# A two-layer decoder trunk: gate projection joined to the value projection, filler rewoven, low halves of weight splits put later

## The chip, the cores and the metric

The kernel runs on one core of one Trainium2 chip. The metric is the device time of one launch in microseconds; several runs of the same kernel are summed up by their median. The profile is one further execution, recorded by the hardware profiler, and its times count from the first instruction of the span. PE is the matrix engine, PEld its weight loads, DVE the vector engine, ACT the scalar engine, POOL the general engine, and SP the engine from whose queue most DMAs are issued.

## The reference, cut to what matters

The trunk has two layers over 512 tokens of width 1024, all in 32-bit floats. Each layer is a mixer, a residual with layer norm, an expert-retrieval feed-forward (PEER, dense over 16384 experts in this kernel), and a second residual with layer norm.

```python
# layer 1, mixer A
proj = x @ w_in                                        # 1024 x (384 q, 384 k, 768 v, 768 r, 16 glr, 256 qm)
log_g = log_sigmoid(glr @ w_gate2 + b_gate) / 16       # low-rank forget gate, rank 16
o = gla_chunked(q / 8, k, v, log_g)                    # 6 heads, chunks of 64 tokens
o = o * rsqrt(mean(o**2) + eps) * head_g * silu(r)
m = softmax(qm @ km.T / 8) @ vm                        # 4 heads over 256 memory tokens; km, vm from mem @ w_mem_kv
mix = concat(o, m) @ w_out
# layer 2, mixer B
q, qm = split(x @ w_in)                                # 12 query heads of 64, 4 memory heads
k, v = split(h @ sb_w_kv)
o = stick_breaking(q, k, v)                            # strictly causal, blocks of 128
mix = concat(o, memory_attention(qm)) @ w_out
```

## The kernel before, in words

**Splits.** A projection in 32-bit floats is made of three matrix products. `split` (line 85) takes a 128 x 1024 weight tile `raw`; ACT copies it, rounded, to `hi`, and DVE subtracts to get `lo`. The tokens x are held in the same way, transposed, as `xhi` and `xlo`: 128 x 8 chunks of the width x 512 tokens. Each block of a product is then hi by hi, hi by lo and lo by hi, accumulated in one PSUM bank. `split` takes an optional list `later`, into which the DVE subtraction is put as a function instead of being issued.

**Two kinds of projection.** `stat_mm` (line 108) holds 128 output columns of the weight and streams tokens: 8 chunks x 3 = 24 matmuls of 512 tokens, the output transposed. `nat_units` (line 154) holds 128 tokens and streams weight columns, with four accumulators for the four token tiles; one `yield` is one unit, that is one 128 x 1024 weight tile. For 512 columns a unit holds two of the eight chunks of the width, 2 x 4 x 3 = 24 matmuls of width 512, and there are four units; for 256 columns it holds four chunks, 48 matmuls of width 256, and there are two units. At the end of the last unit all four accumulators are copied out.

**Buffers.** Raw tiles have four buffers (`RB`, pool `raw`), `hi` and `lo` three each (pool `hl`). In the first mixer there are eight PSUM banks, four with the tag `acc` for `nat_units` and four with the tag `ps` for everything else.

**First mixer** (`mixer_a`, line 393). PE's order is written by hand (`manual_schedule` with PE); the other engines' orders, SP's queue among them, come from the scheduler of the language. At the start the weight block of the gate, padded from 16 to 128 columns, is loaded and split, then x in four loads of 512 KB (`load_xT`, line 443), then 24 matmuls of the gate (line 116 to 118), then eight more blocks (three keys, three queries, two memory queries) with the gate logits in between (`gate_logits`, line 454), then keys and values of the first memory. After that a list of `next(...)` calls (lines 594 to 615) weaves three strands: attention over the memory (`mem`, three steps for each of two pairs of heads: scores, transposes `mpt` at line 362, output `mo`), the preparation of the linear attention (`keys`, `within`), and filler: units of the value projection (`vs`, four units for columns 0 to 511 and two for 512 to 767) and of the second memory's keys and values (`second`, four units). Then come the units of r (`rs_`), with the attention states and outputs between them. The last units' SiLU feeds `scale`, whose result PE transposes (`to_cat`, line 558, matmuls of line 561).

**From layer 1 to layer 2.** The end of `peer` (lines 1521 to 1542) finishes three token tiles; layer norm is on DVE, and `x_to_T` (line 910) transposes a finished tile and splits it. There `more` (line 1526) loads and splits the first three weight blocks (the leads) of the second mixer. The order of PE and DVE is by hand. At the start of `mixer_b` (line 660) the first lead is multiplied by the first 256 tokens (`EARLY`), then `x_to_T` of the last two tiles alternates with `lead_mm` (line 143), which does the other two leads in two pieces; after that all three are multiplied by the other 256 tokens (`LATE`).

**Loop of the second mixer** (lines 852 to 903). Five rounds, each of two heads; PE, DVE and ACT are in the order of the text. A round turns the weights of the heads before (`turn`, transposes on PE, copies to `ez` at line 743), computes logits (matmuls of line 707, DVE minimum of line 710), exponentials on ACT, a scan on DVE (line 725), and fills PE with the projection of blocks for the next round (`stat`). At a round's end `prep` (line 805) loads and splits two weight blocks; their two DVE subtractions are issued together, after the round's last matmuls.

## Time and profile before

| | |
|---|---|
| median of 3 runs | 2904.75 us (2903.73 to 2907.7) |
| the profiled execution | 2906.23 us |
| its span | 2904.4 us |
| PE busy | 2875.8 us, 99% of the span |
| PEld busy | 2550.1 us, 88% |
| DVE busy | 2393.6 us, 82% |
| ACT busy | 1426.6 us, 49% |
| POOL busy | 638.4 us, 22% |

A row of a timeline gives the start in microseconds, the duration, the engine, the line of the code, the operation, the tiles (written <- read), their shape, the count, and in brackets the idle time of that engine before it with what ended it. The duration of a matmul counts to its modelled end, and matmuls overlap: the pace of PE is read from the distance of two starts. A row of waits gives who waited for whom, the sum, the times, and the longest. The first mixer covers about the first 190 us, the second mixer about 1452 to 1636 us.

### The profile page before, as it was taken

The page shows a single profiled execution, that of the slowest core. Times are in us where ns is not written, and L with a number is a line of the kernel's source. Part 1 is how long each engine was busy: PE and PEld are TensorE (multiplying, and loading weights), DVE is VectorE, ACT ScalarE, POOL GpSimd, SP SyncE. Part 2 cuts the span into 40 slices and gives each one's busy share as a digit, 9 for nine tenths or more (in the row PEclk, how much of TensorE's full clock was granted, in tenths as well). Part 3 has the DMA queues.
Part 4 walks back from the last instruction along what each step waited for, and adds up shares of the span by engine and source line. Part 5 has one row for each costly group of instructions (what it writes and reads, how often), then busy time and mean ns, then how long its engine had stood idle before and what let it go on. Part 6 is the DMA issues. An engine that isn't in the chain of part 4 may idle for free.

```text
span 2904.4 us, 44209 instructions
## 1 busy us (share of the span) xinstructions
PE 2875.8 (99%) x16130; PEld 2550.1 (88%) x16130; DVE 2393.6 (82%) x5218; ACT 1426.6 (49%) x2491; POOL 638.4 (22%) x552
## 2 busy tenths in 40 slices
PE   8999999999999999999999999999999999999998
PEld 7878899999999888888886789999999998888886
DVE  5566899999976888888867769999998868888888
ACT  6342447767674333333345524476767743333332
POOL 0110141221322322332100002322212333223320
PEclk9999999999999999999999999999999999999999
DMA  5232488999989999999621325889999999999995
GB/s 198 93 117 65 148 306 310 319 322 327 333 326 325 352 349 352 358 372 353 212 79 51 109 73 175 299 309 324 325 325 330 331 327 347 349 357 365 362 350 179
DMA packets 309531, 791.48 MB, mean 273 GB/s; under 512 B 41904, under 2 KB 127936, under 8 KB 302912
## 3 DMA queue, kind: packets, MB, share of 16 engines
q1 hardware_dynamic: 199296, 416.46, 41.9%
q0 software_dynamic: 73728, 268.47, 26.0%
q10 hardware_dynamic: 36288, 103.72, 9.2%
q8 instruction: 126, 2.06, 0.3%
q14 instruction: 93, 0.76, 0.1%
HBM read 692.88 MB, written 95.68 MB: 272 GB/s over the span
## 4 chain that ended last, share of the span: by engine, by line
PE 95%; DVE 3%; ACT 1%; issue 1%; DMA 1%; DVEq 0%; SPq 0%; ACTq 0%
PE ph L116 13%; PE ph L118 12%; PE ph L117 12%; PE acc L270 11%; PE acc L272 11%; PE acc L274 11%; PE pq L116 2%; PE pq L117 2%; PE pq L118 2%; PE pg L1314 2%; PE pg L1315 1%; PE pss L1372 1%; PE bsp L116 1%; PE bsp L118 1%; PE bsp L117 1%; PE oacc L272 1%
## 5 line engine op out<-in xcount | busy, mean ns | idle before, releaser
L116 PE MATMUL ph<-xhi,uh 128*128 128x384 f32 x2048 | 700.2, 342 | 0.0
L118 PE MATMUL ph<-xhi,ul 128*128 128x384 f32 x2048 | 685.5, 335 | 0.0
L117 PE MATMUL ph<-xlo,uh 128*128 128x384 f32 x2048 | 684.7, 334 | 0.0
L96 ACT ACTIVATE vh<-vr 128x1024 fp32r<-128x1024 f32 x256 | 271.3, 1060 | 543.1 <-issue 356.6
L1042 POOL DMA_INDIRECT gr<-in_un,gidx x256 | 304.8, 1191 | 997.4 <-DVE gr L1077 791.1
L270 PE MATMUL acc<-vh,whi 128*128 128x512 f32 x1536 | 473.7, 390 | 1.3 <-ACT whi L1494 1.3
L272 PE MATMUL acc<-vl,whi 128*128 128x512 f32 x1536 | 473.4, 389 | 0.0
L274 PE MATMUL acc<-vh,wlo 128*128 128x512 f32 x1536 | 473.1, 389 | 0.0
L1042 POOL DMA_INDIRECT gr<-in_vt,gidx x256 | 308.1, 1204 | 735.8 <-DVE va L1095 632.1
L97 DVE TENSOR_TENSOR vl<-vr,vh 128x1024 fp32r<-128x1024 f32 x256 | 313.4, 1224 | 166.7 <-ACT vh L96 166.4
L96 ACT ACTIVATE uh<-ur 128x1024 fp32r<-128x1024 f32 x288 | 304.4, 1057 | 244.9 <-PE ph L117 217.3
L97 DVE TENSOR_TENSOR ul<-ur,uh 128x1024 fp32r<-128x1024 f32 x288 | 350.5, 1217 | 57.6 <-ACT uh L96 57.6
L117 PEld LDWEIGHTS ph<-xlo,uh 128*128 128x128 f32 x2048 | 385.3, 188 | 0.0
L116 PEld LDWEIGHTS ph<-xhi,uh 128*128 128x128 f32 x2048 | 384.9, 188 | 0.0
L118 PEld LDWEIGHTS ph<-xhi,ul 128*128 128x128 f32 x2048 | 384.5, 188 | 0.0
L270 PEld LDWEIGHTS acc<-vh,whi 128*128 128x128 f32 x1536 | 287.7, 188 | 62.5 <-ACT whi L1494 3.0
L272 PEld LDWEIGHTS acc<-vl,whi 128*128 128x128 f32 x1536 | 287.9, 188 | 61.0 <-DVE vl L97 1.5
L274 PEld LDWEIGHTS acc<-vh,wlo 128*128 128x128 f32 x1536 | 287.9, 188 | 60.4 <-DVE wlo L1495 1.0
L1095 DVE SCALAR_TENSOR_TENSOR va<-gr,gw,va 128x1024 f32<-128x1024 f32 x254 | 325.2, 1280 | 7.6 <-DMA gr<-in_vt,gidx 7.2
L1077 DVE SCALAR_TENSOR_TENSOR gr<-gr,xnat 128x1024 f32<-128x1024 f32 x256 | 310.2, 1214 | 12.5 <-DMA gr<-in_un,gidx 12.4
L1287 ACT ACTIVATE obl<-obh,rat 128x128 f16<-128x128 f16 x768 | 244.4, 393 | 24.8 <-ACT gt L1318 6.1
L1494 ACT ACTIVATE whi<-w 128x384 fp32r<-128x384 f32 x256 | 131.0, 512 | 82.4 <-DVE w L1491 82.3
(314 smaller groups left out, 4021.2 us busy)
## 6 DMA issues: line engine op xcount, KB each, us to landing
ur<-in_ut SPq DMA_DIRECT2D x256, 512.0 KB
vr<-in_vt SPq DMA_DIRECT2D x256, 512.0 KB
Gd<-gt ACTq DMA_DIRECT2D x48, 1024.0 KB
Ad<-act ACTq DMA_DIRECT2D x110, 384.0 KB
al<-Ad SPq DMA_DIRECT2D x110, 384.0 KB
gl<-Gd SPq DMA_DIRECT2D x26, 1536.0 KB
ur<-in_wq SPq DMA_DIRECT2D x32, 512.0 KB
bs<-in_b_st SPq DMA_DIRECT2D x14, 512.0 KB
```

The source lines that it names most:

```text
L96: nc.scalar.activation(hi, raw, AF.Copy)
L97: sub = lambda: eng.tensor_sub(lo, raw, hi.bitcast(F32))
L116: nc.tensor.matmul(ps, h, xhi[:, c, sl], start=(c == 0), stop=False)
L117: nc.tensor.matmul(ps, h, xlo[:, c, sl], start=False, stop=False)
L118: nc.tensor.matmul(ps, l, xhi[:, c, sl], start=False, stop=(c == NC - 1))
L270: nc.tensor.matmul(acc[hf], lh, hi[:, hf * 512:(hf + 1) * 512], start=first, stop=False)
L272: nc.tensor.matmul(acc[hf], lh, lo[:, hf * 512:(hf + 1) * 512], start=False, stop=False)
L274: nc.tensor.matmul(acc[hf], ll, hi[:, hf * 512:(hf + 1) * 512], start=False, stop=last)
L1042: nc.gpsimd.indirect_dma_start(out=gr, out_offset=None, in_=tab, in_offset=bass.IndirectOffsetOnAxis(ap=gidx[:, k:k + 1], axis=0))
L1077: nc.vector.scalar_tensor_tensor(gr, gr, 1.0, E.x[:, 0], op0=ALU.mult, op1=ALU.mult, accum_out=gh[:, k:k + 1])
L1095: nc.vector.scalar_tensor_tensor(va, gr, gw[:, k:k + 1], va, op0=ALU.mult, op1=ALU.add)
L1287: nc.scalar.activation(obl[:, q], obh[:, q], AF.Copy, scale=rat[:, n0 + q:n0 + q + 1])
```

## The change

**First mixer, start.** The gate's block is no longer a padded block of its own. Its 16 columns are put beside the value columns 512 to 767 and projected by a new function `values_gates` in units of 272 columns, with tokens held and columns streamed: 8 chunks x 4 token tiles x 3 matmuls. x and these weights are loaded in alternation and in smaller pieces (x: two halves of 256 KB, then three loads of 512 KB; weights: 1, 2, 3 and 2 chunks of 128 x 272). The gate's result lies with the tokens on the partitions, so four PE transposes and a copy are added in `gate_logits`, one step ahead of the logits. Eight blocks follow as before.

**First mixer, filler.** The value strand `vs` now has the four units of columns 0 to 511 alone; the order of the `next(...)` calls is changed accordingly. In `nat_units` the last unit of a chunk goes token tile by token tile, and each accumulator is copied out as soon as it is complete.

**Second mixer, leads.** The low halves of the second and third lead are not subtracted in `more`, but put into a list `E.low` and issued after the first and the second `x_to_T` in `mixer_b`. Accordingly PE does the high-weight products of both leads first (`stat_hi`), and the low-weight products (`stat_lo`) after the second `x_to_T`.

**Second mixer, loop.** Of the two blocks split at a round's end, the first one's low half is issued at once, and the second one's in the next round, after the last logits.

```diff
+def stat_hi(E, ps, hi, lo, sl):
+    for c in range(NC):
+        h = hi[:, c * P:(c + 1) * P]
+        E.nc.tensor.matmul(ps[:, sl], h, E.xhi[:, c, sl], start=(c == 0), stop=False)
+        E.nc.tensor.matmul(ps[:, sl], h, E.xlo[:, c, sl], start=False, stop=False)
+
+def stat_lo(E, ps, hi, lo, sl):
+    for c in range(NC):
+        E.nc.tensor.matmul(ps[:, sl], lo[:, c * P:(c + 1) * P], E.xhi[:, c, sl], start=False, stop=(c == NC - 1))
...
@@ nat_units
+            done = c0 + per == NC
+            steps = [(cc, t) for t in range(nt) for cc in range(per)] if done else [(cc, t) for cc in range(per) for t in range(nt)]
+            for cc, t in steps:
...
-            if c0 + per == NC:
-                for t in range(nt):
-                    evac(ch, t, acc[t][:, :w])
...
+                if done and cc == per - 1:
+                    evac(ch, t, a)
...
@@ mixer_a
+            def values_gates():
+                acc = [psum(E, name="vga", tag="acc") for _ in range(NT)]
+                ws = load_vg(0, 1)
+                load_xT(0, 1)
+                load_xT(1, 1)
+                ws += load_vg(1, 2)
+                load_xT(2, 2)
+                load_xT(4, 2)
+                ws += load_vg(3, 3)
+                load_xT(6, 2)
+                ws += load_vg(6, 2)
+                for c, h, l in ws:
+                    for t in range(NT):
+                        xh, xl = E.xhi[:, c, t * P:(t + 1) * P], E.xlo[:, c, t * P:(t + 1) * P]
+                        nc.tensor.matmul(acc[t][:, :VG], xh, h, start=(c == 0), stop=False)
+                        nc.tensor.matmul(acc[t][:, :VG], xl, h, start=False, stop=False)
+                        nc.tensor.matmul(acc[t][:, :VG], xh, l, start=False, stop=(c == NC - 1))
+                for t in range(NT):
+                    nc.scalar.activation(gl[:, t], acc[t][:, 256:VG], AF.Copy)
+                for t in range(NT):
+                    nc.vector.tensor_copy(v[:, t, 512:], acc[t][:, :256])
...
             def gate_logits():
+                pg = psum(E, name="pgl")
+                for t in range(NT):
+                    nc.tensor.transpose(pg[:16, t * P:(t + 1) * P], gl[:, t], E.ident)
+                nc.scalar.activation(glr[:16], pg[:16], AF.Copy)
+                yield
...
-                glw = split(E, load_raw(E, wst[0], "as"), "as")
-                load_xT()
-                ps = psum(E, name="asp")
-                stat_mm(E, ps, *glw)
-                ev_stat(0, ps)
-                st = stat_units(E, wst, range(1, 9), ev_stat, name="as")
+                values_gates()
+                st = stat_units(E, wst, range(8), ev_stat, name="as")
...
-                vs = nat_units(E, a["a_nat"], [512, 256],
+                vs = nat_units(E, a["a_nat"], [512],
...
                 keys(0)
                 within(0)
+                next(second)
+                next(mem[0])
                 next(vs)
-                next(mem[0])
-                next(second)
                 keys(1)
                 within(1)
+                next(second)
                 next(mem[1])
                 out6()
                 next(vs)
                 next(mem[0], None)
-                next(second)
                 keys(2)
                 within(2)
-                next(vs)
+                next(second)
                 next(mem[1])
-                next(second)
                 next(vs)
                 next(mem[1], None)
                 next(second)
-                next(vs)
...
@@ mixer_b
-                ahead = lead_mm(E, first[1:])
                 with tc.manual_schedule(engines={eng.PE, eng.DVE}):
                     x_to_T(E, E.owed.pop(0), "z")
-                    next(ahead)
+                    E.low.pop(0)()
+                    for p in first[1:]:
+                        stat_hi(E, *p, sl=EARLY)
                     x_to_T(E, E.owed.pop(0), "z")
-                    next(ahead)
+                    E.low.pop(0)()
+                    for p in first[1:]:
+                        stat_lo(E, *p, sl=EARLY)
...
                     next(zz, None)
+                    while low:
+                        low.pop()()
                     exp(h)
...
-                        later = [prep(wst, h + 4) if j < 4 else prep(wnat, 4)]
+                        prep(*((wst, h + 4) if j < 4 else (wnat, 4)))()
                         weights(h + 1)
                         steps(fill)
-                        later.append(prep(wst, h + 5) if j < 4 else prep(wnat, 5))
-                        for f in later:
-                            f()
+                        low.append(prep(*((wst, h + 5) if j < 4 else (wnat, 5))))
...
@@ peer
         def more(k):
-            E.lead.append(split(E, load_raw(E, follow[k], "bs"), "bs"))
+            E.lead.append(split(E, load_raw(E, follow[k], "bs"), "bs", later=E.low if k else None))
```

More of the change, by code (lines that the diff above doesn't have):

```diff
@@ L165, in nat_units @@
             u += 1
-            for cc in range(per):
+            done = c0 + per == NC
+            steps = [(cc, t) for t in range(nt) for cc in range(per)] if done else [(cc, t) for cc in range(per) for t in range(nt)]
+            for cc, t in steps:
                 c = c0 + cc
                 h, l = hi[:, cc * w:(cc + 1) * w], lo[:, cc * w:(cc + 1) * w]
-                for t in range(nt):
-                    xh, xl = xhi[:, c, t * P:(t + 1) * P], xlo[:, c, t * P:(t + 1) * P]
-                    a = acc[t][:, :w]
-                    nc.tensor.matmul(a, xh, h, start=(c == 0), stop=False)
-                    nc.tensor.matmul(a, xh, l, start=False, stop=False)
-                    nc.tensor.matmul(a, xl, h, start=False, stop=(c == NC - 1))
-            if c0 + per == NC:
-                for t in range(nt):
-                    evac(ch, t, acc[t][:, :w])
+                xh, xl = xhi[:, c, t * P:(t + 1) * P], xlo[:, c, t * P:(t + 1) * P]
+                a = acc[t][:, :w]
+                nc.tensor.matmul(a, xh, h, start=(c == 0), stop=False)
+                nc.tensor.matmul(a, xh, l, start=False, stop=False)
+                nc.tensor.matmul(a, xl, h, start=False, stop=(c == NC - 1))
+                if done and cc == per - 1:
+                    evac(ch, t, a)
             yield
@@ L380 @@
 GH = 6
+VG = 256 + 16
 def rsqrt(nc, v, r, q):
@@ L415, in mixer_a @@
             w2 = mp.tile([16, 3, P], F32, name="w2")
+            gl = mp.tile([P, NT, 16], F32, name="gl")
             bgt = mp.tile([P, 16], F32, name="bgt")[:, :3]
@@ L432, in ev_stat, with load_xT @@
             def ev_stat(b, ps):
-                if b == 0:
-                    dst = glr
-                elif b < 4:
-                    dst = kT[:, b - 1]
-                elif b < 7:
-                    dst = qT[:, b - 4]
+                if b < 3:
+                    dst = kT[:, b]
+                elif b < 6:
+                    dst = qT[:, b - 3]
                 else:
-                    dst = qm[:, b - 7]
+                    dst = qm[:, b - 6]
                 nc.scalar.activation(dst, ps, AF.Copy)
-            def load_xT():
-                for c in range(0, NC, 2):
-                    raw = E.x[:, c // 2]
-                    nc.sync.dma_start(raw, a["xT"][c // 2])
-                    hv = E.xhi[:, c:c + 2].rearrange("p c n -> p (c n)")
-                    nc.scalar.activation(hv, raw, AF.Copy)
-                    nc.vector.tensor_sub(E.xlo[:, c:c + 2].rearrange("p c n -> p (c n)"), raw, hv.bitcast(F32))
+            def load_xT(c, n):
+                raw = E.x[:, c // 2, c % 2 * T:c % 2 * T + n * T]
+                nc.sync.dma_start(raw, a["xT"][c // 2][:, c % 2 * T:c % 2 * T + n * T])
+                hv = E.xhi[:, c:c + n].rearrange("p c n -> p (c n)")
+                nc.scalar.activation(hv, raw, AF.Copy)
+                nc.vector.tensor_sub(E.xlo[:, c:c + n].rearrange("p c n -> p (c n)"), raw, hv.bitcast(F32))
@@ new lines, in load_vg @@
+            def load_vg(c, n):
+                raw = E.raw.tile([P, D], F32, tag="raw", name="vg")
+                nc.sync.dma_start(raw[:, :n * VG], a["a_vg"][:, c * VG:(c + n) * VG])
+                hi = E.hl.tile([P, D], F32R, tag="hi", name="vgh")
+                lo = E.hl.tile([P, D], F32R, tag="lo", name="vgl")
+                nc.scalar.activation(hi[:, :n * VG], raw[:, :n * VG], AF.Copy)
+                nc.vector.tensor_sub(lo[:, :n * VG], raw[:, :n * VG], hi[:, :n * VG].bitcast(F32))
+                return [(c + k, hi[:, k * VG:(k + 1) * VG], lo[:, k * VG:(k + 1) * VG]) for k in range(n)]
@@ L850, in mixer_b @@
                     prep(wst, b)()
-                first = {}
+                first, low = {}, []
                 for j in range(1, 6):
```

7 lines of the change are left out of this document (4 added, 3 removed).

## The prediction

> **What bounds the kernel.** I read the page first, then the waits of PE, then the timelines where these waits lie. The page:
>
> ```profile
> span 2904.4 us, 44209 instructions
> PE 2875.8 (99%) x16130; PEld 2550.1 (88%) x16130; DVE 2393.6 (82%) x5218; ACT 1426.6 (49%) x2491; POOL 638.4 (22%) x552
> PE 95%; DVE 3%; ACT 1%; issue 1%; DMA 1%; DVEq 0%; SPq 0%; ACTq 0%
> ```
>
> PE works for 99% of the span and is 95% of the chain that ended last. So the time falls by what PE is spared, by an earlier first matmul, and by each stall of PE that goes, and by little else. The waits of PE in the stages that the diff touches (first mixer; handover to the second mixer; its loop), each with its sum, times and longest:
>
> ```profile
> PE asp L116 <- ACT xhi L449: 7.4, 1, 7.4
> PE ptc L561 <- DVE aT L555: 1.1, 1, 1.1
> PE msc L336 <- DVE aT L503: 0.7, 1, 0.7
> PE xtp L917 <- DVE xlo L922: 1.4, 1, 1.4
> PE bsp L118 <- DVE bsl L97: 0.9, 1, 0.9
> PE pt L739 <- DVE ez L743: 3.4, 8, 0.7
> ```
>
> That is all there is to win outside PE's own work: 7.4 us ahead of the first matmul, 1.8 us inside the first mixer, 2.3 us at the handover, 3.4 us in the loop. The long feed-forward stages are untouched.
>
> **Term 1: the gate's block and the start.** The timeline of PE, with the first matmul, one of those at the slow pace, the first at full pace, the first of block 1, and the first and last of 48 matmuls of width 256:
>
> ```profile
> 7.42 0.80 PE L116 MATMUL asp<-xhi,ash 128*128 128x512 f32 x1 [7.42 <-ACT xhi L449]
> 10.98 0.63 PE L116 MATMUL asp<-xhi,ash 128*128 128x512 f32 x1
> 11.41 0.50 PE L117 MATMUL asp<-xlo,ash 128*128 128x512 f32 x1
> 15.41 0.39 PE L116 MATMUL asp<-xhi,ash 128*128 128x512 f32 x1
> 15.64 0.39 PE L117 MATMUL asp<-xlo,ash 128*128 128x512 f32 x1
> 62.75 0.28 PE L116 MATMUL mkp<-mhl,mkh 128*128 128x256 f32 x1
> 68.29 0.28 PE L118 MATMUL mkp<-mhl,mkl 128*128 128x256 f32 x1
> ```
>
> Width 512 goes at 0.23 us a matmul (15.41 to 15.64), width 256 at (68.29 - 62.75) / 47 = 0.118. Interpolated, width 272 costs 0.118 + 16/256 x 0.109 = 0.125. Before 11.41 the pace is 0.43, nearly half. The seven matmuls from 7.42 to 11.41 took 3.99 where 1.6 would do: 2.4 us lost to the slow pace and one wait.
>
> Today the gate's 24 matmuls end at 15.41, and the 96 matmuls of value columns 512 to 767 cost 96 x 0.118 = 11.3 later. Both together end, in effect, at 26.7. After the change there are 96 x 0.125 = 12.0 us of matmuls at the start. When can they begin? ACT and DVE on the loads:
>
> ```profile
> 5.02 1.06 ACT L96 ACTIVATE ash<-as 128x1024 fp32r<-128x1024 f32 x1 [1.52 <-DMA as<-in_a_st]
> 6.31 1.06 ACT L449 ACTIVATE xhi<-xnat 128x1024 fp32r<-128x1024 f32 x1 [0.23 <-DMA xnat<-in_xT]
> 10.23 1.06 ACT L449 ACTIVATE xhi<-xnat 128x1024 fp32r<-128x1024 f32 x1 [0.22 <-DMA xnat<-in_xT]
> 11.32 1.23 DVE L450 TENSOR_TENSOR xlo<-xnat,xhi 128x1024 fp32r<-128x1024 f32 x1
> 81.65 0.60 PE L490 MATMUL pk<-ident,kk 128*128 128x128 f32 x4
> 82.18 1.16 PE L500 MATMUL pa<-qT,kk 64*128 64x128 f32 x16
> ```
>
> Loads of 512 KB land 1.3 us apart ((10.23 - 6.31) / 3). The first weight piece is 139 KB, a quarter: it lands about 1.0 us before 5.0, the 256 KB of x 0.65 after that, at 4.7; its copy takes about 0.6 (half of 1024 columns at 1.06, and a fixed part), so PE starts at about 5.4 instead of 7.42. With 12.0 of work and again 2.4 for the slow pace and the first waits it ends at 19.8. Do loads or splits hold it up? x and weights are 2.1 + 1.1 MB; at 512 KB in 1.3 us the 3.1 MB behind the first piece take 7.7, so the last lands by 12, and its splits, in a chain of DVE at 1.23 us per 1024 columns, end by about 14; the last two chunks are due at 19.8 - 3.0 = 16.8. So they are covered by 2.8 us. The four gate transposes cost as those of the keys, 82.18 - 81.65 = 0.53; the copies of the results (ACT and DVE) lie under the block of matmuls that follows. Gain: 26.7 - 19.8 - 0.5 = 6.4. Ends: 8.0 if the slow pace ends at once, 4.5 if pieces come late by 2 us. SP's queue has more and smaller loads ahead of the next block's; that block is due at 19.8, some 8 us after the last piece, which covers its landing and its split, so I put nothing down. The gate logits come one block (5.4 us) later; the keys that need them come as late as 81.65, so nothing either.
>
> The Trainium skill ("DMA: Bandwidth & Descriptors", section on bandwidth) advises transfers of 1 MiB and more for three quarters of the peak, and speaks against cutting these loads; by that rule the cut loads run slower and the sum below would be nearer 9 than 12. Today's 512 KB loads, at 1.3 us each (about 400 GB/s), show no such loss, and the smaller sizes are in no row here.
>
> **Term 2: filler.** The 0.7 us at `msc` is there since scores of the second pair come right after `within(1)`, whose banks DVE has still to empty. Now a unit of the second memory's keys (24 matmuls, 2.8 us) lies between: gain 0.7. What is shortened is the way from the first pair's scores to its transposes: a unit of 5.4 us (24 x 0.23) leaves it and one of 2.8 enters, 2.6 less. The last step of softmax, and the first copy of the transposes today:
>
> ```profile
> 81.91 1.37 DVE L355 TENSOR_SCALAR mp<-mp,msm 128x256 f32<-128x256 f32 x5
> 89.49 0.69 DVE L364 COPY mpT<-mpt 128x512 f32<-128x512 f32 x1 [2.88 <-PE mpt L362]
> ```
>
> The weights are ready at 83.3, the transposes begin some 0.6 ahead of their copy, at 88.9: 5.6 us of slack cover the 2.6. A new wait arises with the second pair: the first value unit of the second memory now comes before its transposes and keeps two of the four `ps` banks until its second unit. Four transposed tiles then share two banks, and the third waits for a copy of 0.69: loss 0.5 (ends 0 and 1.7, with another 1.2 of a split queued ahead on DVE). The wait of 1.1 at `ptc` goes: SiLU and scaling of three of four token tiles now run while the last unit is still on PE. Gain 1.1 (ends 0 and 1.1), as the chain of output weights behind starts at the last transpose. Term 2: 0.7 + 1.1 - 0.5 = 1.3.
>
> **Term 3: the leads.** DVE first, then PE:
>
> ```profile
> 1452.85 1.43 DVE L97 TENSOR_TENSOR bsl<-bs,bsh 128x1024 fp32r<-128x1024 f32 x1
> 1458.46 1.22 DVE L97 TENSOR_TENSOR bsl<-bs,bsh 128x1024 fp32r<-128x1024 f32 x1
> 1461.89 1.28 DVE L922 TENSOR_TENSOR xlo<-xtp,xhi 128x512 fp32r<-128x512 f32 x2
> 1462.63 1.97 PE L917 MATMUL xtp<-ident,xnat 128*128 128x128 f32 x8 [1.45 <-DVE xlo L922]
> 1464.25 0.56 PE L116 MATMUL bsp<-xhi,bsh 128*128 128x256 f32 x1
> ```
>
> Here DVE is the bound. Without the two subtractions the two `xlo` of line 922 start 2.4 us earlier, at 1459.5, and the transposes, which wait for the first of them, at about 1460.2 instead of 1462.63. But the subtractions come back behind: `xlo` to 1460.8, first subtraction to 1462.0, `xlo` of the last tile to 1463.2, second subtraction to 1464.4. `stat_lo` of the last lead (8 x 0.12) then ends at 1465.4; today the 12 matmuls left after 1464.25, the first at half pace, end near 1466.1. DVE's total is the same, so only its idle time is won: about 0.75. PE's waits are moved (0.75 ahead of the transposes, 0.7 and 1.45 ahead of the two `stat_lo`: 2.9 us), not removed. What such gaps do to the clock, in the view by windows (third number from the end is the granted clock):
>
> ```profile
> 1458.67:1462.08 3.41, 1.60 (x12) 1.25 (x10) 3.24 (x9) 0.00 (x0) 0.00 (x0) 1.00 0.38 111
> 1462.08:1465.49 3.41, 2.86 (x14) 2.86 (x15) 2.01 (x4) 1.20 (x2) 0.00 (x0) 0.53 0.11 46
> 1550.83:1554.24 3.41, 2.56 (x16) 1.31 (x13) 3.41 (x7) 0.60 (x1) 0.00 (x0) 1.00 0.48 159
> 1554.24:1557.65 3.41, 3.41 (x12) 2.72 (x11) 1.51 (x4) 2.17 (x2) 0.00 (x0) 0.53 0.01 2
> 1571.31:1574.72 3.41, 2.56 (x18) 1.40 (x16) 2.89 (x4) 0.49 (x1) 0.00 (x0) 1.00 0.19 44
> ```
>
> After a window in which PE worked 1.60 of 3.41 us the next ran at half clock. Moved gaps can do the same, and the half-clocked stretch would then be dense matmuls: up to 1.7 us lost (half of 3.41), against at most 1.4 today (half of 2.86). I take a gain of 0.3 (ends +0.75 and, with today's loss hidden behind the transposes' waits, 0.75 - 1.7 = -0.9).
>
> The Trainium skill ("TensorE: Matmul & The Clock Gate", on the HAM clock gate) puts windows of 3413 ns on a free-running grid, as here, but lets the clock fall only after a window of idling. By that rule no piece of the 2.9 us would slow the clock and term 3 would be 0.75. The trace disagrees: 47% busy was enough, and once 75%.
>
> **Term 4: the loop.** One round:
>
> ```profile
> 1549.94 1.23 DVE L812 TENSOR_TENSOR bsl<-bs,bsh 128x1024 fp32r<-128x1024 f32 x1 [1.83 <-ACT bsh L810]
> 1551.82 0.44 PE L739 MATMUL pt<-ident,zs 128*128 128x128 f32 x2 [0.69 <-DVE ez L743]
> 1558.06 2.83 DVE L725 TENSOR_TENSOR_SCAN ez<-go,ez 128x1280 f32<-128x1280 f32 x1 [2.31 <-ACT ez L720]
> 1541.65 2.37 PE L753 MATMUL pav<-ez,v 128*64 128x512 f32 x16
> 1583.87 2.37 PE L753 MATMUL pav<-ez,v 128*64 128x512 f32 x16
> 1604.22 2.15 PE L753 MATMUL pav<-ez,v 128*64 128x512 f32 x12
> ```
>
> The second subtraction stands ahead of two copies that free the banks for PE's next transposes. Put behind the logits it falls into DVE's 2.31 us of idling before the scan, which covers its 1.23; if that cover were gone, each of four rounds would pay up to 1.23. Its block is due only after the next block's 24 matmuls. So the 8 waits go: gain 3.4. The first of these rounds also had the half-clocked window from 1554.24: two rounds took 1583.87 - 1541.65 = 42.2, a later one 20.35, so 1.5 more. The same 2.56 of work in 1571.31 had no such effect; without the gaps it is less likely. I put half of it, 0.8 (ends 0 and 1.5).
>
> **Sum.** 6.4 + 1.3 + 0.3 + 3.4 + 0.8 = 12.2 us. The profiled execution took 2906.23 (span 2904.4), 1.5 above the median 2904.75; so 2894.0 for such an execution, and 2892.5 for the median. The upper ends add to 8.0 + 1.8 + 0.75 + 3.4 + 1.5 = 15.5, the lower ones to 4.5 - 1.0 - 0.9 + 3.4 + 0 = 6.0: the forecast's own range is 2889.3 to 2898.7.
>
> **Rivals.**
> *More is won* (0.12): slow pace short at the start and no half-clocked window behind: 12.2 + 1.6 + 0.5 + 0.7 = 15, 2889.7. For it: both windows follow gaps. Against it: the grid's place is chance.
> *Pieces land late* (0.05): the cut loads run at half of today's rate; the 7.7 us become 15.4, the last split ends near 21 and the stage with two chunks near 23: 12.2 - 3.2 = 9, 2895.7. Against it: 512 KB loads follow each other at an even 1.3 us. The Trainium skill's rule on transfer size (page above) would lead here.
> *The loop's wait returns* (0.09): the late subtraction delays minimum or scan, and terms 3 and 4 give nothing: 7.7, 2897. Against it: 2.31 us of idling.
> *The rewoven filler does not fit* (0.06): bank and split waits eat 3.5 of the first mixer's gain: 8.7, 2896. For it: two banks for four tiles, and shorter units between dependent steps.
> *The first stage starves* (0.10): its matmuls wait for pieces chunk by chunk and the clock stays half; 96 x 0.25 = 24 us instead of 14.4: 12.2 - 9.6 = 2.6, 2902. The gate then saves nothing since it ran under the loads anyway, and the change doesn't do what it says. For it: PE today ends the gate only 5 us behind the last load's copy (10.23). Against it: four times the matmuls per chunk are more cover.
> *Slower* (0.04): the same starving goes on into the key blocks, whose splits wait for the buffers that the pieces hold; each block at half pace costs 24 x 0.2 = 4.8 more. From the first such block on the kernel is slower than before; with two, 12.2 - 9.6 - 9.6 = -7: 2911.8. Against it: those buffers come free from the third chunk on, some 8 us ahead of need.
>
> **Numbers.** The forecast has 0.54. A measurement of this kernel tells about 0.2%, 5.8 us, from no change: faster means below 2898.9. Forecast, more, late pieces, loop and filler lie there: 0.86. Starving is the same: 0.10; slower 0.04. The range 2888 to 2899.5 takes in the ends of the forecast, with about 1 us at each side for the runs' own spread (2903.73 to 2907.7), and leaves out the last two cases.
>
> **What would show it.** Right: first matmul near 5.4 us; no matmuls of a padded gate block; the first key block near 20; no wait of `pt` on `ez` and rounds of about 19.5 us; `xtp` near 2.4 us earlier against its stage, `bsp` waiting for `bsl` instead. Wrong: the stage of 272 columns ending after 24; waits of PE on loads; `mpt` or `msc` waits above 2 us; the loop's rounds unchanged, with a wait on `zs` in place of `ez`.

## The result and the profile after

The changed kernel takes 2890.82 us, the median of 6 runs (2888.65 to 2891.42), against 2906.9 us for the kernel before (6 runs, 2903.73 to 2907.7). The ratio is 0.9946, with a 95% interval of 0.9933 to 0.9959: faster by 0.54%, or 11.9 to 19.5 us. The profiled spans are 2904.4 and 2889.4 us, 15.0 apart. The forecast was 2892.5 us, and the range 2888 to 2899.5.

The page of the kernel after:

```profile
span 2889.4 us, 44181 instructions
PE 2866.8 (99%) x16110; PEld 2543.5 (88%) x16110; DVE 2392.4 (83%) x5220; ACT 1427.4 (49%) x2497; POOL 639.7 (22%) x552
```

PE is busy for 9.0 us less and the span is 15.0 us shorter. PE is still the bound at 99%.

The waits of PE in the kernel after: the first mixer (0 to 215 us), the handover (1444 to 1465), and the second mixer's loop with its end (1520 to 1640), one fence for each:

```profile
PE vga L490 <- ACT xhi L462: 5.7, 1, 5.7
PE oacc L286 <- DVE wol L100: 0.6, 1, 0.6
PE oacc L284 <- DVE cat L205: 0.5, 1, 0.5
PE mpt L376 <- DVE mpT L378: 0.3, 1, 0.3
```

```profile
PE bsp L132 <- DVE bsl L97: 1.6, 2, 1.1
PE xtp L965 <- DVE xlo L970: 0.6, 1, 0.6
```

```profile
PE oacc L284 <- ACT woh L96: 0.8, 1, 0.8
PE oacc L286 <- DVE wol L97: 0.5, 1, 0.5
```

The waits at `ptc` and `msc` are gone, and so are all eight of `pt` on `ez`. A small one at `mpt` is new, and so are two of 1.1 us together at the first output projection (`oacc`); the stretch from there on is no longer than before all the same, as the table below shows. In the handover the sum stays near what it was (2.2 us against 2.3), with other names.

Where the time came from is read by the positions of the same work in both traces. The first matmul, the first block of keys, the first matmul after the attention steps and the first accumulator matmul of the first output projection, in the kernel after:

```profile
5.70 0.59 PE L490 MATMUL vga<-vgh,xhi 128*128 128x272 f32 x1 [5.70 <-ACT xhi L462]
20.79 0.40 PE L116 MATMUL asp<-xhi,ash 128*128 128x512 f32 x1
131.47 0.40 PE L187 MATMUL ara<-arh,xhi 128*128 128x512 f32 x1
183.82 0.48 PE L284 MATMUL oacc<-woh,cat 128*128 128x512 f32 x1
```

and the last two in the kernel before:

```profile
137.15 0.40 PE L172 MATMUL ara<-arh,xhi 128*128 128x512 f32 x1
190.94 0.70 PE L270 MATMUL oacc<-woh,cat 128*128 128x512 f32 x2
```

The start columns give: 5.7 us won by `ara` (137.15 - 131.47), 7.1 by `oacc`. The same reading further on gives the table; each row is the difference of the two traces between two landmarks.

| stretch | before, us | after, us | won, us |
|---|---|---|---|
| start to first `ara` | 137.15 | 131.47 | 5.7 |
| `ara` to first `oacc` | 53.79 | 52.35 | 1.4 |
| `oacc` to the first feed-forward's second stage (`acc`) | 735.2 | 735.0 | 0.2 |
| that stage | 525.6 | 527.0 | -1.3 |
| leads: first `bsp` to first `pt` | 77.60 | 76.44 | 1.2 |
| loop: first `pt` to first `oacc` | 106.90 | 98.07 | 8.8 |
| the rest | 1268.1 | 1269.1 | -1.0 |

The stretches of the feed-forward are not touched by the change. In the traces of the experiments the stage with -1.3 takes between 525.6 and 531.1 us, whatever is edited, and "the rest" between 1267.6 and 1269.1; the losses there are such scatter. The 1.2 won at the leads and 1.5 of the 8.8 won in the loop are no gain of the change either, as the experiments show.

### The profile page after: what moved, and what is told of

Read it like the earlier page. It is cut to its first block, busy times and chain, and to the rows that moved or that the text cites. A ratio compares the mean times of both kernels' runs of the same rounds, so it can differ in the third digit from the quotient of the medians.

```text
span 2889.4 us, 44181 instructions
## 1 busy us (share of the span) xinstructions
PE 2866.8 (99%) x16110; PEld 2543.5 (88%) x16110; DVE 2392.4 (83%) x5220; ACT 1427.4 (49%) x2497; POOL 639.7 (22%) x552
```

## The experiments

**Each part alone.** Three kernels were built from the kernel before with one part of the change each: the loop's order, the leads' order, the whole of the first mixer.

```diff
# loop_only, on the kernel before
+                    while low:
+                        low.pop()()
...
-                        later = [prep(wst, h + 4) if j < 4 else prep(wnat, 4)]
+                        prep(*((wst, h + 4) if j < 4 else (wnat, 4)))()
...
-                        later.append(prep(wst, h + 5) if j < 4 else prep(wnat, 5))
-                        for f in later:
-                            f()
+                        low.append(prep(*((wst, h + 5) if j < 4 else (wnat, 5))))
```

> The kernel before with the change of the second mixer's loop alone. Theory A, each stall is worth its distance of starts: a round of the loop goes from 20.3 us to 18.6 us between the starts of its pav groups, four rounds give 7.1 us, and with the half-clocked stretch of the first round gone (1.5 us) the gain is 7 to 9 us, ratio 0.997. Rival B, a stall is worth its row in the list of waits: 3.4 us, with the half-clocked stretch at most 4.9, and the rest of what the whole change won in the loop came from the other parts shifting where the clock's windows fall: rounds near 19.5 us.

```diff
# lead_only, on the kernel before (with stat_hi and stat_lo as in the change)
-                    next(ahead)
+                    E.low.pop(0)()
+                    for p in first[1:]:
+                        stat_hi(E, *p, sl=EARLY)
...
-            E.lead.append(split(E, load_raw(E, follow[k], "bs"), "bs"))
+            E.lead.append(split(E, load_raw(E, follow[k], "bs"), "bs", later=E.low if k else None))
```

> The kernel before with the change of the second mixer's leads alone. Theory A: PE's waits are moved, DVE's idling of about 0.75 us is won; the transposes xtp start about 2.4 us earlier in their stage, and 0.6 to 0.8 us and 1.1 to 1.5 us are waited for the low halves. Gain 0.75 us, or 1.2 to 1.5 if no half-clocked window follows. Rival B: the moved gaps slow the clock in the matmuls of the late tokens, up to 1.7 us lost: gain 0 or a loss of up to 0.9 us. Both lie near the limit of what the timing can tell; the traces decide by the distance from the first bsp to the first pt of the loop: 77.6 us before, 76.4 with the whole change.

```diff
# first_only, on the kernel before: all that the change does in mixer_a and nat_units
+                values_gates()
...
```

> The kernel before with the change of the first mixer alone (gates with the values, smaller loads, rewoven filler, copies out per token tile). Theory A: the three parts add; the output projection starts 7.1 us earlier (190.9 to 183.8 us), gain 6.5 to 7.5 us, ratio 0.9975. The rounds of the loop stay at 20.3 us. Rival B: part of the second mixer's gain is owed to the shift in time; then this kernel alone shows the half-clocked stretches after 1452 us gone and gains 8.5 to 10 us.

Measured, in medians against 2904.69 us for the kernel before, measured with them (19 runs): the loop alone 2897.9, ratio 0.9974 (0.9964 to 0.9985); the leads alone 2904.68, ratio 0.9998 (0.9988 to 1.0007); the first mixer alone 2896.55, ratio 0.9969 (0.9957 to 0.9981). The product of the three is 0.9941, inside the interval of the whole change.

How long a round of the loop is shows in the first product with the values of each round. The kernel before has such rows at 1583.87 and 1604.22, 20.35 apart. With the loop's order alone:

```profile
1540.65 2.37 PE L753 MATMUL pav<-ez,v 128*64 128x512 f32 x16
1559.21 2.38 PE L753 MATMUL pav<-ez,v 128*64 128x512 f32 x16
```

18.56 us a round. Each of four rounds gave 1.8 us (the last and longest one went from 27.63 to 25.66, or 2.0), although the list of waits held 3.4 us for all of them together. Lead alone has 20.31 to 20.36, first mixer alone too. So Theory A of loop_only holds for the rounds. For the first mixer alone, Theory A gives the size (its output projection starts at 183.62).

Its Rival B is right in one thing: both half-clocked windows behind 1452 us are missing from its trace, though neither leads nor loop were touched. The window in the first round of the loop (21.89 us there instead of 20.33) stands in the trace of the kernel before alone. Three other kernels have the old rounds, and the loop takes 105.33 to 105.36 us in them (lead_only, first_only, second_at_end) against 106.90. So the new order of the loop is worth 105.35 - 98.07 = 7.3 us. The other 1.5 us are the chance of where the clock's windows fall. The median of loop_only, 6.8 us below that of the kernel before, agrees.

**Where the 1.8 us of a round were.** A round of the kernel before, DVE and PE between two blocks of fill (the third column is the busy time of the row; rows of PE group several matmuls):

```profile
1570.06 1.03 PE L739 MATMUL pt<-ident,zs 128*128 128x128 f32 x8
1571.83 1.22 DVE L812 TENSOR_TENSOR bsl<-bs,bsh 128x1024 fp32r<-128x1024 f32 x1 [3.07 <-ACT bsh L810]
1572.98 1.28 DVE L743 COPY ez<-pt 128x512 f32<-128x512 f32 x2
1574.91 1.29 PE L707 MATMUL pz<-kq 64*128 64x256 f32 x4
1576.13 0.50 PE L116 MATMUL bsp<-xhi,bsh 128*128 128x512 f32 x1
```

and the same in the kernel after:

```profile
1578.16 1.03 PE L784 MATMUL pt<-ident,zs 128*128 128x128 f32 x8
1578.80 1.29 DVE L788 COPY ez<-pt 128x512 f32<-128x512 f32 x2 [0.93 <-PE pt L784]
1581.85 0.70 PE L752 MATMUL pz<-kq 64*128 64x256 f32 x4
1582.49 0.50 PE L116 MATMUL bsp<-xhi,bsh 128*128 128x512 f32 x1
```

From the first `pt` to the next fill PE needs 6.07 us before (1576.13 - 1570.06) and 4.33 after. In the row before the copy DVE stood idle for 3.07 us (1.83 to 1.87 in the other rounds). It had the subtraction next in its order, and that waits for ACT's `bsh`; behind it stood the copies, which in the kernel after follow 0.64 us behind the first `pt`. Part of PE's loss has no idle row at all: the last four `pz` take 1.29 us before and 0.70 after, with no idle time noted in front. They are products of half the array's rows, two heads side by side. After, the two of a pair start 7 ns apart, and the second pair 0.32 us behind the first; before, all four start about 0.3 us apart (1574.911, 1575.231, 1575.508, 1575.828). The first and the third start 0.05 us after DVE's minimum has emptied a bank of `pz` (1574.856 and 1575.454), and the other two 0.32 us behind them. So PE waits for banks here, as far as the starts tell, and the profile counts that as busy.

Two kernels put back a part of the old order, to tell which of the two, the wait for ACT or the subtraction itself, costs the time:

```diff
# second_at_end, on the changed kernel
-                        low.append(prep(*((wst, h + 5) if j < 4 else (wnat, 5))))
+                        prep(*((wst, h + 5) if j < 4 else (wnat, 5)))()
```

> The changed kernel with the second low half of each loop round issued at the round's end again (the first stays where the change put it). Theory A, the second one alone is the stall, since DVE stands in its queue for ACT's copy (1.8 us) and then subtracts (1.2 us) ahead of the two copies that PE needs: rounds of 20.3 us again, total 7 us longer than with the whole change, DVE idle about 1.8 us ahead of that subtraction. Rival B, it was both subtractions back to back, 2.4 us of DVE: with the first one early the round gets about half of it back, 19.4 us.

```diff
# early_hi, on the changed kernel
                         weights(h + 1)
+                        second = prep(*((wst, h + 5) if j < 4 else (wnat, 5)))
+                        second()
                         steps(fill)
-                        low.append(prep(*((wst, h + 5) if j < 4 else (wnat, 5))))
```

> The changed kernel, but in the loop the second block's copy on ScalarE is put ahead of the last matmuls that fill, and its subtraction follows directly, ahead of the copies that the matmuls wait for, as in the order before. Theory A (the stall was VectorE standing in order until ScalarE's copy had ended): a round takes about 18.6 us, though the subtraction is ahead of the copies. Rival B (the 1.2 us of VectorE ahead of the copies is itself the stall): 19.4 us or more, up to the 20.3 of the kernel before.

second_at_end has rounds of 20.35, 20.31, 20.35 and 27.63, the same as the kernel before has outside its half-clocked window, and the same row in the list of waits:

```profile
PE pt L784 <- DVE ez L788: 3.4, 8, 0.7
```

So the second subtraction alone makes the stall; the first may stay where it was. (Its one time, 2902.08 us, is not read: the untouched feed-forward stage of its trace took 531.1 us instead of 527.) In early_hi ACT's copy is early, so the subtraction starts as soon as it is DVE's turn, but still ahead of the copies:

```profile
1552.89 2.38 PE L798 MATMUL pav<-ez,v 128*64 128x512 f32 x16
1571.92 2.38 PE L798 MATMUL pav<-ez,v 128*64 128x512 f32 x16
1578.45 1.03 PE L784 MATMUL pt<-ident,zs 128*128 128x128 f32 x8
1578.93 1.23 DVE L860 TENSOR_TENSOR bsl<-bs,bsh 128x1024 fp32r<-128x1024 f32 x1 [0.55 <-ACT bsh L858]
1580.07 1.28 DVE L788 COPY ez<-pt 128x512 f32<-128x512 f32 x2
1583.23 0.50 PE L116 MATMUL bsp<-xhi,bsh 128*128 128x512 f32 x1
```

A round takes 19.03 us: neither theory's number. The delay of the copies behind the first `pt` orders the three kernels: 0.64 us after (1578.80 - 1578.16), 1.62 in early_hi, 2.92 before. From `pt` to the next fill PE takes 4.33, 4.78 and 6.07. The first 1.0 us of delay costs 0.45, the next 1.3 cost all of 1.3. So of the 1.8 us a round, about 1.3 were DVE standing in order for ACT's copy, and about 0.5 the subtraction itself. The list of waits for this window of early_hi has not one row of PE, though each round loses nearly half a microsecond: here all of it lies inside busy time.

How much cover has the new place? One kernel does the late subtraction three times over:

```diff
# cover3, on the changed kernel
-                        low.pop()()
+                        f = low.pop()
+                        for _ in range(3):
+                            f()
```

> The changed kernel with the late low half subtracted three times over (same result), 2.4 us more of DVE in each of four rounds, at the place behind the logits. Theory A, the idling of 2.3 us ahead of the scan covers the first subtraction and most of a second, and the scan's result is due some 5 us after it is ready: rounds stay at 18.6 us within 0.1. Rival B, the cover is used up by the one: rounds grow by up to 2.4 us, to 21.

The rounds are 18.57, 18.66, 18.65 and 26.99, against 18.57, 18.57, 18.57 and 25.66. Another 2.4 us of DVE is hidden in three rounds, to 0.1 us. The last, which has less fill, pays 1.3; `pt` waits there 1.0 us for ACT's `zs`. One subtraction is covered in all four.

**The leads.** lead_only had no effect on the time. Its trace shows the half-clocked window that the prediction feared; by windows (bounds, length, busy time of PE, PEld, DVE, ACT and POOL, then the granted clock, the share of DMA and its rate):

```profile
1463.61:1467.02 3.41, 1.82 (x14) 1.38 (x13) 3.11 (x4) 1.00 (x2) 0.00 (x0) 1.00 0.47 143
1467.02:1470.43 3.41, 3.41 (x18) 3.41 (x18) 0.00 (x0) 0.00 (x0) 0.00 (x0) 0.50 0.52 171
```

PE worked 1.82 of 3.41 us, and the next window ran at half clock. In the kernel after the grid lay otherwise across the same gaps. Counted in windows of 3.413 us from its own change of clock at 11.59 us, the emptiest window of the stage and the one behind it are:

```profile
1455.43:1458.84 3.41, 1.86 (x13) 1.66 (x14) 2.71 (x4) 0.59 (x1) 0.00 (x0) 1.00 0.44 155
1458.84:1462.25 3.41, 3.41 (x30) 3.41 (x30) 0.00 (x0) 0.00 (x0) 0.00 (x0) 1.00 0.45 155
```

No half clock there, with 0.04 us more work in the window. Over all fourteen traces the half-clocked window stands in this stage in seven, in old and new order alike. Sorted by it, the stage (first `bsp` to first `pt`) takes: without it 76.35 and 76.41 us in the old order (first_only, loop_only), 76.44 to 76.56 in the new one (five traces); with it 77.60 in the old (the kernel before) and 77.93 to 78.00 in the new (six traces). So the new order of the leads is worth nothing, rather 0.1 to 0.4 us slower, and the 1.2 us between the two main traces are the chance of the grid. The Trainium skill ("TensorE: Matmul & The Clock Gate", Part 1) ties the half rate to an idle window; in these traces windows with PE busy for half their time (1.82 of 3.41 us) were followed by it.

**The first stage.** It ends at 20.79 us; the forecast was 19.8. Is it the clock (full only from 11.6 us on), the late first matmul, or the splits? Four kernels ask.

```diff
# warm, on the changed kernel
+                warm = psum(E, name="warm")
+                for k in range(20):
+                    nc.tensor.transpose(warm[:, k % 4 * P:(k % 4 + 1) * P], E.ident, E.ident)
+                nc.vector.tensor_copy(E.junk1, warm[:, :1])
```

> The changed kernel with 20 transposes of the identity on PE ahead of the first stage, from about 1.6 us on, while the first loads are under way. Theory A, the first stage pays for the slow pace: its 25 matmuls from 5.7 to 11.6 us at 0.227 instead of 0.127 lose 2.5 us, and with the clock up early the stage ends 1 to 2.5 us sooner than 20.7; gain over the changed kernel 1 to 2.5 us. Rival B, the stage is paced by the splits of the pieces, not by the clock: the stage ends within 0.5 us of 20.7 and waits on xlo or vgl appear in its place.

```diff
# whole_loads, on the changed kernel
-                ws = load_vg(0, 1)
-                load_xT(0, 1)
-                load_xT(1, 1)
-                ws += load_vg(1, 2)
+                ws = load_vg(0, 3)
+                load_xT(0, 2)
                 load_xT(2, 2)
...
```

> The changed kernel with the first stage's loads uncut: x in four loads of 512 KB, the weights in three (3, 3 and 2 chunks). Theory A: cut pieces bring the first matmul forward and cost no rate; uncut, the first matmul comes at about 7.2 us instead of 5.7, the stage ends at about 21.5 to 22.2 instead of 20.7, total 1 to 1.5 us longer. Rival B, larger transfers run faster: the last piece lands earlier than with cut loads, and the stage ends no later than 20.7.

`whole_warm` is both at once, with 24 transposes:

> The changed kernel with its first loads whole (not cut into pieces) and 24 transposes of the identity on TensorE ahead of the first matmul. Theory A (with whole loads the splits come in time, VectorE's last one at 14.1 us, and only the clock and the late first matmul kept the stage long): the first block of keys begins at 19.5 to 20.2 us, against 22.16 with whole loads alone and 20.79 in the changed kernel. Rival B (something else of the first stage, loads or splits, paces it): 20.7 us or later. The time is the changed kernel's within 2 us either way.

```diff
# recut_warm: warm, and the third piece of the weights cut in two
                 load_xT(2, 2)
+                ws += load_vg(3, 1)
                 load_xT(4, 2)
-                ws += load_vg(3, 3)
+                ws += load_vg(4, 2)
```

> The changed kernel with the third piece of the weights cut into one chunk and two, the first ahead of the x chunks 4 and 5, and 20 transposes of the identity on TensorE first. Theory A (the split of the third piece of the weights paces chunk 3): chunk 3 starts at about 12.1 us instead of 13.2 and the first block of keys begins at 19.6 to 20.0. Rival B (the splits of x, ScalarE or the loads pace it in any cut): 20.7 or later. The time is the changed kernel's within 2 us.

| kernel | first matmul of the product, us | full clock from | chunk 3 begins | first block of keys |
|---|---|---|---|---|
| after (cut loads) | 5.70 | 11.6 | 13.23 | 20.79 |
| warm (cut) | 5.78 | 7.2 | 12.62 | 20.89 |
| whole_loads | 6.91 | 12.5 | 14.60 | 22.16 |
| whole_warm | 6.80 | 4.5 | 12.57 | 20.14 |
| recut_warm | 5.21 | 4.6 | 12.93 | 21.67 |

With cut loads the clock changes next to nothing. In warm PE has the full clock 4.4 us earlier, waits 1.2 us on `vgl` and `xlo`, and ends no sooner: Rival B of that run holds. In the kernel after, PE waits for nothing behind its first matmul, so there the slow pace itself is what holds it up to 11.6 us; but the splits stand close behind. DVE in the kernel after:

```profile
9.58 2.51 DVE L463 TENSOR_TENSOR xlo<-xnat,xhi 128x1024 fp32r<-128x1024 f32 x2 [1.64 <-ACT xhi L462]
12.01 0.22 DVE L446 CAST msk<-mf 128x128 uint8<-128x128 f32 x1
12.15 1.00 DVE L472 TENSOR_TENSOR vgl<-vg,vgh 128x816 fp32r<-128x816 f32 x1
13.22 1.23 DVE L463 TENSOR_TENSOR xlo<-xnat,xhi 128x1024 fp32r<-128x1024 f32 x1
14.36 0.72 DVE L472 TENSOR_TENSOR vgl<-vg,vgh 128x544 fp32r<-128x544 f32 x1
```

The low half of the third weight piece ends at 13.15. Chunk 3 starts at 13.23, needs that half first in its third matmul, at 13.48, and five chunks of 1.51 us end at 20.79. Six other kernels have the same first stage (first_only, second_at_end, cover3, evac_at_end, old_order, early_hi). In them and in warm the first block of keys begins 7.44 to 7.47 us behind the end of this split (12.96 to 13.42), though their clock is full anywhere from 7.2 to 11.3 us. In the kernel after it begins 7.64 behind. So the slow pace costs 0.2 us there, and the split of the third piece holds the rest. With whole loads and a warm clock (whole_warm) PE waits in the first chunk alone:

```profile
PE vga L492 <- ACT xhi L462: 1.0, 1, 1.0
PE vga L493 <- DVE xlo L463: 0.9, 1, 0.9
```

and its stage ends at 20.14, earliest of all. That is Theory A of that run. recut_warm went the other way: the piece that was moved back came late (PE waits 1.3 us on `vgh` and 1.1 on `vgl`), and the stage ended at 21.67, so its Theory A falls. The rate of the loads goes with this. The DMA's rate in 40 slices of the first 16 us, in the kernel after and then in whole_loads:

```profile
GB/s 0 0 0 0 45 180 386 339 145 139 205 284 341 362 326 395 338 369 379 416 383 366 404 401 383 444 379 409 418 437 385 430 399 430 297 205 154 348 338 287
```

```profile
GB/s 0 0 0 0 90 85 214 309 414 424 421 390 329 370 401 357 446 392 436 391 436 367 419 401 396 420 410 410 410 410 410 410 410 338 389 389 348 389 369 297
```

A slice is 0.4 us. Where the cut pieces are under way (slices 9 to 12, 3.2 to 4.8 us) the rate is 139 to 284 GB/s against 390 to 424 with whole loads. Summed to 8 us that is 1.86 MB against 2.19 MB, or 0.8 us at 410 GB/s. The two warm kernels moved 1.69 and 2.19 MB in that time, which would make 1.2 us, and their ends lie 0.75 apart: the rate gives the direction, and not the size. The Trainium skill ("DMA: Bandwidth & Descriptors", section on bandwidth) advises transfers of 1 MiB and more for three quarters of the peak; these rows agree so far as the pieces of 136 to 272 KB were slow, but the loads of 512 KB already ran at about 410 GB/s. Whether the size or the issue of more loads sets the lower rate was not told apart. Still, the cut loads are the better choice with the cold clock (20.79 against 22.16), since PE starts earlier. whole_warm as a whole is not faster than the changed kernel (2891.69 us, one run): its 0.65 us, and 1.4 more, go at the first output projection. PE waits 1.9 us for DVE there, as in all three kernels with a warm-up, which costs warm and recut_warm 0.5 us by the end of that projection; old_order, without a warm-up, waits 1.7 us at the same place, and what brings this wait is not shown. In whole_warm alone a half-clocked window follows, from 185.37 to 188.78 us, behind a window in which PE worked 1.51 of 3.41 us. The medians (warm 2890.04, ratio 0.9946, 0.9933 to 0.996; one time each of whole_loads, 2892.69, and recut_warm, 2891.91) lie within 2 us of the changed kernel's, below what a measurement tells. So do the single times of cover3 (2892.48), early_hi (2892.24), evac_at_end (2890.91) and old_order (2889.21): all these kernels are read by positions.

**The filler.** Two kernels put back half of it each: the old order of copying out in the last unit, and the old order of the strands.

```diff
# evac_at_end, on the changed kernel
-            steps = [(cc, t) for t in range(nt) for cc in range(per)] if done else [(cc, t) for cc in range(per) for t in range(nt)]
+            steps = [(cc, t) for cc in range(per) for t in range(nt)]
...
-                if done and cc == per - 1:
-                    evac(ch, t, a)
+            if done:
+                for t in range(nt):
+                    evac(ch, t, acc[t][:, :w])
```

> The changed kernel with the last unit of a chunk in the old order (chunk by chunk, all four accumulators copied out at the end). Theory A: the wait of the transposes ptc on the scaled heads comes back, 1.1 us by the list of waits, 1.4 us from the end of the last unit of r to the first matmul of the output projection (3.1 instead of 1.7 us). Rival B: the wait had gone because the earlier strands had moved, and it stays away.

```diff
# old_order, on the changed kernel
-                next(second)
-                next(mem[0])
                 next(vs)
+                next(mem[0])
+                next(second)
                 keys(1)
...
```

> The changed kernel with the filler of the first mixer's attention drawn in the old order, without the two units that the gates no longer need. Theory A (the new weave is worth a little): the wait ahead of the second msc is back and the stretch from msc to the last gate transpose is 51.9 to 52.5 us against 51.41. Rival B (what the new weave wins ahead of msc it loses ahead of the mpt matmuls): 51.4 within 0.2. The time is the changed kernel's within 1.5 us for both.

evac_at_end, where the last `ptc` and the first `oacc` stand:

```profile
184.88 0.33 PE L613 MATMUL ptc<-ident,aT 128*128 128x128 f32 x1 [1.06 <-DVE aT L607]
184.96 0.70 PE L285 MATMUL oacc<-woh,cat 128*128 128x512 f32 x2
```

The wait of the kernel before is back, and from the last product of the unit to `oacc` PE takes 3.18 us against 1.78: 1.4 us are shown for this edit. In old_order the wait ahead of the second `msc` is back:

```profile
100.72 1.12 PE L350 MATMUL msc<-KmT,qm 64*128 64x256 f32 x8
102.51 1.92 PE L350 MATMUL msc<-KmT,qm 64*128 64x256 f32 x8 [0.67 <-DVE aT L554]
121.93 1.91 PE L376 MATMUL mpt<-ident,mp 128*128 128x128 f32 x16
```

yet the stretch from the first `msc` to the first `ara` is 51.41 us there and 51.41 in the kernel after, whose rows are:

```profile
104.16 2.50 PE L350 MATMUL msc<-KmT,qm 64*128 64x256 f32 x16
118.74 1.04 PE L376 MATMUL mpt<-ident,mp 128*128 128x128 f32 x8
120.13 1.12 PE L376 MATMUL mpt<-ident,mp 128*128 128x128 f32 x8 [0.35 <-DVE mpT L378]
```

The second `msc` took 3.71 us with its wait (102.51 + 1.92 - 100.72) and takes 2.50. The second `mpt` took 1.91 and takes 2.51 (120.13 + 1.12 - 118.74), and the first rose by 0.26. So the new weave wins 1.2 us at `msc`, loses 0.9 of it at the `mpt` banks, and the last 0.3 in no single row: the whole is nothing, as Rival B had it.

## Why the prediction was right, point by point

**Bound, size and sign.** The forecast of 12.2 us held: 15.0 by the spans, 16.1 by the medians (13.9 against the 19 later runs of the kernel before), 11.9 to 19.5 by the interval. What PE is spared and each stall that goes are what the time fell by, as the prediction began. Its terms fared unevenly, and 2.7 of the 15.0 us are luck: the trace of the kernel before has two half-clocked windows (1.2 and 1.5 us) that come and go without the change.

**Term 1 (6.4 forecast, 5.7 measured).** The stage ended at 20.79, not 19.8: in the sum's own terms the first matmul came at 5.70 instead of 5.4 (at 4.64 to 5.78 in the other kernels with cut loads), the slow pace and the first waits took 3.0 instead of 2.4, and the work 12.1 instead of 12.0. The step that failed is "so they are covered by 2.8 us". It is true for the last two chunks (their splits end at 15.08, due at 17.77), but the middle piece is the tight one: its low half ends 0.33 us ahead of the matmul that takes it. So the slow pace, put into the sum as the reason for the end, is not what decides it: in warm the clock was full 4.4 us earlier and the end the same, and without the slow pace the kernel after would have gained 0.2 us. That the sum came near is luck, since the split of the middle piece holds PE back about as long. The two removed units measured 5.84 and 5.75, the forecast's 11.3 within 0.3; the transposes cost 0.53, as forecast.

**Term 2 (1.3 forecast, 1.4 measured, for other reasons).** The `ptc` gain was 1.4 (forecast 1.1). The 0.7 at `msc` came, even 1.2, and the price at the two banks was not 0.5 but, with what is in no single row, the whole of it. The row of waits at `mpt` names 0.3; the rest lies in busy time.

**Term 3 (0.3 forecast, 0 measured).** The gaps were forecast as 0.75, 0.7 and 1.45 us; beyond the pace of the matmuls they measured 0.76, 0.64 and 1.28. The step that failed is "only its idle time is won: about 0.75": sorted by the clock, the stage is not shorter in the new order. The gaps are as long in all as they were: in loop_only, old order at full clock, PE's two gaps measure 1.08 and 1.61, or 2.69 us, and the three of the kernel after 2.68. DVE's idle time of 0.78 us lies behind them there, at 1463.33, where PE has its next matmuls and waits for nothing. The half-clocked window behind the moved gaps was foreseen with its size (up to 1.7; measured 1.2 to 1.6); it comes in half of the traces. (The prediction's window with 1.60 us of work has 1.45 when it is laid on the clock's own grid, 0.2 us later; nothing hangs on the difference.)

**Term 4 (3.4 + 0.8 forecast, 8.8 measured, 7.3 of it by the change).** The mechanism was right, the size was off by a factor of two. The failing step is "So the 8 waits go: gain 3.4": the price of a stall was read from the list of waits, 0.85 us a round, where the starts of the same matmul in successive rounds give 1.8; four rounds make 7.3. The rest, 1.5, is the half-clocked window of the first round (21.89 against 20.33), of which the sum took half. The reason given for it, that the window is less likely without the gaps, is not borne out: three traces with the same gaps do not have it. The cover of 2.31 us of DVE's idling was enough, as put; after the change 1.18 of it are left.

**What balanced it.** 5.7 + 1.4 + 0.2 + 8.8 are 16.1, and 1.2 of the leads' clock window come to it; -1.3 and -1.0 in stages that the change leaves alone bring it to 15.0. Without the two clock windows the parts of the change are worth 5.7 + 1.4 + 7.3 = 14.4 us by positions: the loop gave 3.9 more than forecast, and the other terms 1.7 less. Of the rivals, *more is won* names the right side and nearly the size, but the early end of the slow pace that it rested on did not bring it. *The loop's wait returns* and *the first stage starves* did not come: the slow pace ended at 11.6, as before, and no wait of PE on a piece is left in the list behind the first. *Pieces land late* had the direction: the cut loads ran slower for a while, and the last split ended at 15.08 instead of 14, but not at 21.

Not settled is why `acc` of the first feed-forward takes 525.6 to 531.1 us from one trace to the next; no run was aimed at it. The longest, second_at_end, has this row there, against 0.6 us for the same row in both main kernels:

```profile
PE acc L284 <- ACT whi L1542: 4.1, 3, 3.4
```

A half-clocked window follows its wait of 3.4 us. What made that copy late is open.

## What to carry to other kernels

Price a stall of a loop by the starts of the same matmul in successive rounds, or by PE's time from one landmark to the next, and not by the list of waits: late banks also stretch rows that count as busy. An instruction that waits on another engine in an in-order queue holds all behind it, so look at what stands behind it whose data are there; putting it after them, under an idle stretch, costs nothing as long as that stretch is longer than it. When one wait is moved by reordering filler, compare a whole stretch with and without the reordering, since what leaves one place can come back at another.

## What the runs showed of the hardware

A window of the clock's grid in which PE worked about half the time or less can be followed by one at half clock. Counted from each trace's own change of clock, nine windows in which PE worked 0.92 to 1.83 of 3.41 us were followed by half clock: seven at the leads, one in whole_warm at 181.96, one in second_at_end at 932.45. Windows with 1.86 (the kernel after) and 1.88 (loop_only) were not. Two readings do not fit a plain limit in busy time: 1.75 in whole_warm at 4.46 was not followed by it, and 2.56 in the first round of the loop was, in the kernel before, while fifteen such windows with 2.56 in four traces were not. The 1.2 to 1.6 us that a window costs at the leads or in the loop come and go with the place of the grid.

Transposes of the identity, with nothing else on PE, bring the clock up. In whole_warm they run from 1.6 us on, at 0.21 us each, and at 0.11 from 4.46 us on, where the clock is full. In recut_warm it is full at 4.64, also ahead of the first matmul of the product; in warm at 7.18, 1.4 us behind it. In the kernel after it is full at 11.6, 5.9 us behind the first matmul.
